# Ordering DVE and SP work in a hybrid attention/RWKV block: the next weight's lower part behind a read-out, and weight loads free of gate loads in the second branch

## The chip, the cores and the metric

The kernel runs on one core of a Trainium2 chip. A core has five engines that run side by side, each with its own instruction stream taken in order: TensorE (PE in the profile, with its weight loads as PEld), VectorE (DVE), ScalarE (ACT), GpSimd (POOL) and SyncE (SP), which here only issues DMA transfers. Data lies in HBM and is brought into the on-chip memory (SBUF) by DMA; matmuls write into the accumulator memory (PSUM). The metric is the device time of one execution in microseconds: 1654.64 us is the median of three runs before the change, with 1653.51 the lowest and 1662.36 the highest.

## The reference

One transformer-like block on a sequence of 1024 tokens of 1024 features, in float32:

```
mod = silu(c) @ w_mod + b_mod            # six shift/scale/gate vectors
u   = rms_norm(x) * (1 + scale1) + shift1
proj = u @ w_in                          # fox q,k,v,f | rwkv r,k,v,w,a,g | two gates
o_fox  = softmax(q k^T / 8 + forget decay, causal) v        # 8 heads of 64
p = p_rwkv + (token_shift(p_rwkv) - p_rwkv) * mu
o_rwkv = RWKV-7 recurrence(r, k, v, w, a, g)                # 8 heads of 64
mix = (sigmoid(p_gate0) * (o_fox @ fox_w_out) + sigmoid(p_gate1) * (o_rwkv @ rwkv_w_out)) @ w_o
h = x + gate1 * mix
h = h + gate2 * (silu(conv3(u2 @ w_up_a)) * (u2 @ w_up_b)) @ w_down
out = rms_norm(h) * final_g
```

The projections are the bulk of the work: u (1024 x 1024) times w_in (about 5,400 columns), the two output projections, w_o and the feed-forward part.

## The kernel before

**Split numbers.** Every float32 operand of a large matmul is split into a high part (rounded to the matmul's faster format) and a lower part (the rest). A product is three passes: high x high, high x low, low x high. For a weight tile the order is: weight-high with u-high (8 matmuls, one for each 128 features), weight-high with u-low (8), weight-low with u-high (8). So 24 matmuls of 512 columns make one half (512 tokens) of 128 output features, and the weight's lower part is first needed at the 17th.

**Weights, one after the other.** `load_w` (line 257 on) issues the DMA of a 128 x 1024 weight tile into a raw buffer (two of them), lets ACT copy it into the high part (L272) and DVE subtract to get the lower part in two instructions of 512 columns (L274). High and lower parts have two buffers each, so weight i+1's parts can be written while weight i is in use, once weight i-1 is through with them; the raw buffer of weight i is free for weight i+2 when its lower part is made. `Weave.step` drives this: when it makes a weight the current one, it loads the next one at once, and only then writes down the current one's matmuls.

**Users of the weights.** `shifted` makes one half of one r, k or v tile of RWKV: 24 matmuls into one of two PSUM banks (tag "big"), an ACT instruction that scales the result by mu (L366), and the read-out by DVE (L369), which adds the token-shifted part and frees the bank. Each of these 24 weight uses takes its own weight load, since the two halves are made at different times. `qk_steps` makes both halves of a q or k tile with one weight: ACT takes the high part (L393), DVE the lower part (L395, name ql), and six DMAs write them to HBM. `v_steps` uses two weight tiles at once for the attention's v, in eight 24-matmul pieces with 256 columns each, whose lower part is L955. `gate_steps` makes the gates (L337 to L342) and writes them to HBM (d_gate).

**What sets the order.** The order of PE's instructions is written out by hand over the whole kernel (`tc.manual_schedule` for PE): `Weave` has an estimated clock and puts projection matmuls between the steps of two chains, the preparation of an RWKV unit (`pre`) and its recurrence (`main`). DVE, ACT, POOL and SP are ordered in this stage by a planner that goes through the instructions in the order written, estimates when each is ready, and takes the earlier-written one among those that are ready; semaphores then follow from the data. `tc.add_manual_dep(a, b, NOSYNC)` tells the planner to put a behind b on their engine, without a semaphore. Among what DVE does beside the read-outs are 31 steps of two small operations for each RWKV unit (L784, L786) and the transposes X (L842), which wait for a DMA round trip through HBM.

**The branches.** After attention, the kernel forms gate x (output projection) for the two branches x = 0 (fox) and x = 1 (rwkv), eight tiles n each (`br_part`: 12 matmuls for each half). For tile k = 8x+n+1, `br_open` copies the weight (L1219 ACT; L1222 POOL for the lower part) and loads the gate g from d_gate (L1224, two buffers, free when DVE has used the tile two before, L1314 or L1317); `br_load` then issues the load of tile k+1's weight (L1210) into one of the two raw buffers. `after_gate` puts the load behind the last gate load in SP's order. In the second branch, w_o tiles are loaded and split too (L1287, L1258, L1259), and the last two modulation vectors are accumulated on DVE from w_mod (L1274, L1281), in both branches.

Of the kernel before, what the change touches and what calls it, by code (L numbers as in the profile page):

```python
# [12 lines left out]
ALU = mybir.AluOpType  # L13
# [5 lines left out]
NH = 512  # L19
# [16 lines left out]
NOSYNC = mybir.DependencyInfo(mybir.DependencyClass.NoSync, mybir.DependencyReason.DATA)  # L36
# [96 lines left out]
def hybrid_block(ctx: ExitStack, tc: tile.TileContext, a, out):  # L133
    nc = tc.nc
# [12 lines left out]
    def f32(ap):  # L147
        return ap.bitcast(F32)

    tt, stt, ts = nc.vector.tensor_tensor, nc.vector.scalar_tensor_tensor, nc.vector.tensor_scalar  # L150
# [15 lines left out]
    def V(name, i=0, n=1):  # L166
        o, _ = VEC[name]
        return vec[:, o + i : o + i + n]
# [13 lines left out]
    omu = cp.tile([128, 14], F32, name="omu")  # L182
# [59 lines left out]
            nc.vector.tensor_tensor(dst[:, cs], ps, bb[:, cs], op=ALU.add)  # L242

    marks = {}
    late_lo = deque()

    def lower(wait=0):

        yield wait
        if late_lo:  # L250
            hi, lo, raw = late_lo.popleft()
            for c in range(0, 1024, NH):
                tt(lo[:, c : c + NH], raw[:, c : c + NH], f32(hi[:, c : c + NH]), op=ALU.subtract)
            weave.use("DVE", weave.now, 1300)

    def load_w(src, name, pool=None, n=1024, scale=None, tags=("whi", "wlo"), bufs=2):

        pool = pool or wp
        raw = rp.tile([128, n], F32, tag="raw", name=f"raw_{name}")
        nc.sync.dma_start(raw, src)  # L260
        if scale is not None:
            nc.gpsimd.tensor_tensor(raw, raw, scale, op=ALU.mult)
        hi = pool.tile([128, n], F32R, tag=tags[0], name=f"hi_{name}", bufs=bufs)
        lo = pool.tile([128, n], F32R, tag=tags[1], name=f"lo_{name}", bufs=bufs)
        if weave.late == 1:
            i = nc.gpsimd.tensor_copy(hi, raw)
            if "head" in marks:
                tc.add_manual_dep(i.ins, marks["head"].ins.name, NOSYNC)
            late_lo.append((hi, lo, raw))
            weave.spawn(lower(9000), 0)  # L270
        else:
            nc.scalar.copy(hi, raw)  # L272
            for c in range(0, n, NH):
                nc.vector.tensor_tensor(lo[:, c : c + NH], raw[:, c : c + NH], f32(hi[:, c : c + NH]), op=ALU.subtract)  # L274
        return hi, lo

    def gemm_cm(ps, w, x, cs, nk=KT, w0=0):
# [7 lines left out]
    def gemm_steps(ps, w, x, cs, nk=KT, w0=0, by_kt=False):  # L285
        (wh, wl), (xh, xl) = w, x
        order = [(i, kt) for i in range(3) for kt in range(nk)]
        if by_kt:
            order.sort(key=lambda o: o[1])
        for n, (i, kt) in enumerate(order):  # L290
            ww, xx = ((wh, xh), (wh, xl), (wl, xh))[i]
            k0 = (w0 + kt) * 128
            mm(ps, ww[:, k0 : k0 + 128], xx[:, kt, cs], start=n == 0, stop=n == len(order) - 1)
            yield
# [29 lines left out]
    def w_in(i):  # L324
        return load_w(a["w_in"][i], f"in{i}")
# [20 lines left out]
    with ExitStack() as es:  # L346
# [4 lines left out]
        def big(name):  # L351
            return pb.tile([128, NH], F32, tag="big", name=name)
# [4 lines left out]
        def shifted(w, ti, hf, dst, prev, name, by_kt=False):  # L357

            ps = big(f"ps_{name}{hf}")
            yield from gemm_steps(ps, w, u, slice(hf * NH, hf * NH + NH), by_kt=by_kt)  # L360
            sh = shp.tile([128, NH + 1], F32, tag="sh", name=f"sh_{name}{hf}")
            if hf == 0:
                nc.vector.memset(sh[:, 0:1], 0.0)
            else:
                nc.vector.tensor_copy(sh[:, 0:1], prev)
            nc.scalar.activation(sh[:, 1 : NH + 1], ps, AF.Copy, scale=V("mu", ti))  # L366
            if hf == 0:
                nc.gpsimd.tensor_copy(prev, sh[:, NH : NH + 1])
            stt(dst, ps, omu[:, ti : ti + 1], sh[:, 0:NH], op0=ALU.mult, op1=ALU.add)  # L369

        rkv, got, last_col = {}, {}, {}

# [13 lines left out]
        def qk_steps(w, i):  # L386
            sc_ = 0.125 if i < 4 else 1.0
            for hf in range(2):
                cs = slice(hf * NH, hf * NH + NH)
                ps = big(f"qk{i}_{hf}")  # L390
                yield from gemm_steps(ps, w, u, cs)
                hi = gsp.tile([128, NH], F32R, tag="sp0", name=f"qh{i}_{hf}")
                nc.scalar.activation(hi, ps, AF.Copy, scale=sc_)  # L393
                lo = gsp.tile([128, NH], F32R, tag="sp0", name=f"ql{i}_{hf}")
                stt(lo, ps, sc_, f32(hi), op0=ALU.mult, op1=ALU.subtract)  # L395
                h0 = 2 * (i % 4)
                for t, k, r0 in ((hi, 0, 0), (lo, 0, 64), (hi, 2, 0)) if i < 4 else ((hi, 1, 0), (hi, 1, 64), (lo, 3, 0)):
                    for h in range(2):
                        nc.sync.dma_start(f32(d_st[h0 + h, k, r0 : r0 + 64, cs]), f32(t[h * 64 : h * 64 + 64, :]))
# [13 lines left out]
        with tc.tile_pool(name="st", bufs=1) as st, tc.tile_pool(name="stp", bufs=2, space=PS) as stp, \  # L413
# [126 lines left out]
            for half in range(2):  # L540
                for kt in u_steps(half):
                    low_part(kt, half, (0, 1))
                    if half == 0 and kt in (3, 5):
                        raw, hi, lo = low_raw[kt == 5]
# [13 lines left out]
        with tc.tile_pool(name="lg", bufs=1, reuse_waits="tile") as lg, \  # L558
# [108 lines left out]
            for p in range(4):  # L667
                for i in (p, 4 + p):
                    weave.add(lambda i=i: w_in(i), lambda w, i=i: qk_steps(w, i))
# [288 lines left out]
        for j in range(2):  # L958
            weave.add(lambda j=j: [load_w(a["w_v"][j, x], f"v{j}{x}") for x in range(2)], lambda w, j=j: v_steps(w, j))
# [226 lines left out]
    def bank(k, name):  # L1186
        return pb.tile([128, NH], F32, tag="big", name=name) if k > 5 else pz.tile([128, NH], F32, tag=f"p{k}", name=name)
# [16 lines left out]
    def after_gate(i):  # L1204
        if "g" in marks:
            tc.add_manual_dep(i.ins, marks["g"].ins.name, NOSYNC)

    def br_load(x, n):
        raw = br_raw[x, n] = rp.tile([128, 1024], F32, tag="raw", name=f"raw_br{x}{n}")[:, 0:NH]
        after_gate(nc.sync.dma_start(raw, a["w_br"][n, :, x * NH : x * NH + NH]))  # L1210

    def br_open(x, n):
        if (x, n) not in br_raw:
            br_load(x, n)
        raw = br_raw[x, n]
        hi = br.tile([128, NH], F32R, tag="whi", name=f"hi_br{x}{n}")
        lo = br.tile([128, NH], F32R, tag="wlo", name=f"lo_br{x}{n}")
        if x or n:
            marks["br"] = nc.scalar.copy(hi, raw)  # L1219
        else:  # L1220
            nc.gpsimd.tensor_copy(hi, raw)
        nc.gpsimd.tensor_tensor(lo, raw, f32(hi), op=ALU.subtract)  # L1222
        g = br.tile([128, S], F32, tag="g", name=f"g{x}_{n}")
        marks["g"] = nc.sync.dma_start(g, d_gate[8 * x + n])  # L1224
        opened[x, n] = (hi, lo), g
# [3 lines left out]
    if "rest" in marks:  # L1229
        g, m = (gsp.tile([128, NH], F32, tag="sp0", name=f"rest{k}") for k in range(2))  # L1230
        i = nc.scalar.activation(g, marks["rest"], AF.Abs)
# [89 lines left out]
    for x in range(2):  # L1321
        for n in range(8):
            if x or n:
                k = 8 * x + n + 1
                if k < 16:
                    br_open(k // 8, k % 8)
                if k < 15:
                    br_load((k + 1) // 8, (k + 1) % 8)
            parts = [(x, n, 0), (x, n, 1)]
            if x == 0 and n < 2:  # L1330
                parts = [(0, 0, 0), (0, 1, 0)] if n == 0 else [(0, 0, 1), (0, 1, 1)]
            for _ in range(0 if x and n > 3 else 1 if x else 2 if n < 6 else 0):
                next(mods, None)
            for part in parts:
                br_part(*part)
            if x == 0 and 1 <= n <= 4:
                rk_make((n - 1) // 2 * 2, (n - 1) % 2)
            if x == 1:
                wo_load(n)
                if n == 0:  # L1340
                    lo = [hp.tile([128, NH], F32R, tag=tag, name=f"mgl0_{k}", bufs=bufs)
                          for k, (tag, bufs) in enumerate(5 * [("xq", 5)] + 2 * [("s", 2)] + [("dg", 1)])]
                    mg_hl[0] = pairs([f"f{k}" for k in range(4)], "mgh0"), lo
                else:
                    mg_split(0, n - 1)
# [299 lines left out]
    ps = {t: [bank(k, f"wo{t}_{c}") for c, k in enumerate(ks)] for t, ks in enumerate(((0, 5), (6, 7), (1, 2)))}  # L1645
# [13 lines left out]
    def wo_do(t, k):  # L1659
        ps = [bank(k + c, f"wo{t}_{c}") for c in range(2)]  # L1660
        for kt in range(KT):
            wo_mm(t, kt, ps)
        return ps

    ps = wo_do(3, 3)
# [7 lines left out]
    ps = wo_do(4, 0)  # L1673
# [15 lines left out]
    for t, k in ((5, 2), (6, 6), (7, 4)):  # L1689
        ps = wo_do(t, k)  # L1690
# [234 lines left out]
    for s, k in enumerate(ORDER):  # L1925
        ps = banks[4:] if k in (7, 4, 2) else banks[0:4]
# [109 lines left out]
```

## Time and profile before

| what | us |
|---|---|
| median of three runs | 1654.64 |
| the profiled execution, its own time | 1657.87 |
| its span, first to last instruction | 1656.1 |
| TensorE busy in the span | 1610.4 |
| weight loads of TensorE busy | 1340.5 |
| DVE busy | 1221.4 |
| ACT busy | 821.6 |
| lower parts of w_in tiles on DVE (L274), 84 instructions | 57.7 |

The stages lie one behind the other: the first norm and the low-rank projections up to about 130 us; projections with the RWKV recurrence to about 627; attention with the last gates to 827; the two branches to 918; w_o and the second norm to about 1063; the feed-forward part to the end. In the rows of the profile, "out<-in" are the names of tiles, "x8" the number of instructions merged into a row, and "[2.78 <-DVE v L369]" says that the engine stood idle for 2.78 us just before and that the read-out of v by DVE at line 369 ended it. Idle time of an engine that is not the bottleneck costs nothing by itself. "SPq" rows are transfers at the moment that SP issues them.

### The profile page before, as it was taken

How to read it: one execution, taken by the hardware profiler on the slowest of the kernel's cores; microseconds unless marked ns; L12 is line 12 of the kernel's file. 1: busy time of each engine (PE TensorE's matmuls, PEld its weight loads, DVE VectorE, ACT ScalarE, POOL GpSimd, SP SyncE). 2: the span in 40 equal slices, each digit the busy share in tenths (PEclk: the TensorE clock that was granted, in tenths of full speed). 3: DMA queues.
4: the chain of work that ended last, by engine and by line, in shares of the span. 5: the costliest groups of instructions: out<-in, count | busy, mean ns of one | idle time of the engine just before them, and what ended most of it. 6: DMA issues, size and time to landing. Idle time of an engine off the chain costs nothing.

```text
span 1656.1 us, 25949 instructions
## 1 busy us (share of the span) xinstructions
PE 1610.4 (97%) x9694; PEld 1340.5 (81%) x9694; DVE 1221.4 (74%) x2373; ACT 821.6 (50%) x1537; POOL 133.5 (8%) x153
## 2 busy tenths in 40 slices
PE   7999999999999999999999999999999999999998
PEld 7777777897878788888887888788888888888886
DVE  5786787878876636888778447897777777886677
ACT  5563335445455655666633225644444444555455
POOL 0010101111111011221031000000000000000000
PEclk9999999999999999999999999999999999999999
DMA  9487645443333336434197421243223233674463
GB/s 337 139 322 233 178 122 140 125 122 104 100 115 97 96 114 165 125 105 124 35 358 242 184 85 43 77 134 102 96 97 119 96 99 106 212 264 157 123 210 108
DMA packets 121645, 240.59 MB, mean 145 GB/s; under 512 B 40048, under 2 KB 48880, under 8 KB 121520
## 3 DMA queue, kind: packets, MB, share of 16 engines
q1 hardware_dynamic: 113040, 220.58, 40.8%
q0 software_dynamic: 8480, 18.37, 4.2%
q8 instruction: 76, 1.25, 0.3%
q14 instruction: 49, 0.40, 0.1%
HBM read 173.35 MB, written 65.54 MB: 144 GB/s over the span
## 4 chain that ended last, share of the span: by engine, by line
PE 61%; DVE 5%; ACT 2%; DMA 2%; issue 1%; SPq 0%; POOL 0%; ACTq 0%; DVEq 0%
PE X L141 13%; PE D L141 13%; PE Y L141 6%; PE wo L141 5%; PE gt L141 5%; PE rk_ps L141 4%; PE W L141 3%; PE br L141 3%; PE lg L141 2%; PE ov L141 2%; PE tp L145 2%; PE ps_rkv L141 1%; DMA raw_wo<-in_w_o 1%; DVE nm L1049 1%; DVE P L1059 1%
## 5 line engine op out<-in xcount | busy, mean ns | idle before, releaser
L141 PE MATMUL D<-op,op 128*128 128x512 f32 x924 | 209.8, 389 | 0.0
L141 PEld LDWEIGHTS D<-op,op 128*128 128x128 f32 x924 | 173.4, 188 | 36.2 <-DVE op L1259 0.3
L141 PE MATMUL X<-T_m,S 128*128 128x512 f32 x440 | 107.8, 390 | 1.6 <-ACT T_m L1720 1.1
L141 PEld LDWEIGHTS X<-T_m,S 128*128 128x128 f32 x440 | 82.4, 188 | 20.4 <-ACT T_m L1720 2.5
L1258 ACT CAST op<-g 128x512 fp32r<-128x512 f32 x77 | 47.8, 621 | 73.7 <-PE D L141 48.8
L1259 DVE TENSOR_TENSOR op<-g,op 128x512 fp32r<-128x512 f32 x77 | 53.0, 689 | 41.3 <-ACT op L1258 41.3
L1517 DVE SCALAR_TENSOR_TENSOR c<-ab,vec,c 128x512 f32<-128x512 f32 x88 | 65.9, 750 | 18.4 <-ACT c L1520 16.8
L784 DVE TENSOR_TENSOR t<-E,M 128x60 f32<-128x60 f32 (+24 forms) x248 | 56.5, 228 | 26.5 <-DMA M<-sm 20.5
L274 DVE TENSOR_TENSOR lo_in<-raw_in,hi_in 128x512 fp32r<-128x512 f32 x84 | 57.7, 725 | 20.8 <-PE gt L141 7.2
L1483 DVE TENSOR_TENSOR A<-ur,A 128x512 fp32r<-128x512 f32 x64 | 44.0, 689 | 38.7 <-ACT A L1479 38.5
L1483 DVE TENSOR_TENSOR S<-ur,S 128x512 fp32r<-128x512 f32 x66 | 45.5, 691 | 35.2 <-ACT S L1479 35.1
L1479 ACT CAST S<-ur 128x512 fp32r<-128x512 f32 x66 | 41.0, 622 | 55.8 <-DVE ur L1472 30.6
L141 PE MATMUL Y<-T_h,A 128*128 128x512 f32 x264 | 63.7, 390 | 0.3 <-ACT T_h L1720 0.3
L141 PE MATMUL Y<-T_h,S 128*128 128x512 f32 x264 | 63.6, 390 | 0.4 <-ACT T_h L1738 0.4
L1053 ACT ACTIVATE P<-lg,nm 128x896 f32<-128x896 f32 (+3 forms) x64 | 47.5, 744 | 28.6 <-DVE nm L1049 19.6
L1479 ACT CAST A<-ur 128x512 fp32r<-128x512 f32 x64 | 39.6, 622 | 43.1 <-PE X L141 31.3
L786 DVE TENSOR_TENSOR E<-E,t 128x60 f32<-128x60 f32 (+24 forms) x248 | 55.9, 225 | 6.4
L141 PE MATMUL W<-B_f,A 128*128 128x512 f32 x252 | 60.6, 389 | 0.0
L141 PE MATMUL X<-B_b,A 128*128 128x512 f32 x252 | 60.5, 389 | 0.0
L141 PEld LDWEIGHTS Y<-T_h,S 128*128 128x128 f32 x264 | 49.5, 188 | 11.1 <-ACT T_h L1738 0.8
L141 PEld LDWEIGHTS Y<-T_h,A 128*128 128x128 f32 x264 | 49.5, 188 | 11.0 <-ACT T_h L1720 0.7
L1089 DVE TENSOR_TENSOR tl<-tp,th 128x512 fp32r<-128x512 f32 (+1 forms) x80 | 49.4, 633 | 9.2 <-ACT th L1086 8.5
(483 smaller groups left out, 4132.4 us busy)
## 6 DMA issues: line engine op xcount, KB each, us to landing
raw_in<-in_w_in SPq DMA_DIRECT2D x50, 512.0 KB, 3.9
wm<-in_w_mod SPq DMA_DIRECT2D x48, 512.0 KB, 7.2
ur<-in_w_up SPq DMA_DIRECT2D x44, 512.0 KB, 3.8
g<-d_g SPq DMA_DIRECT2D x35, 512.0 KB, 4.0
d_g<-gs SPq DMA_DIRECT2D x44, 256.0 KB, 2.0
d_g<-c SPq DMA_DIRECT2D x33, 256.0 KB, 4.5
d_st<-qh SPq DMA_DIRECT2D x64, 128.0 KB, 2.4
stA<-d_st POOLq DMA_DIRECT2D x8, 1024.0 KB, 6.7
```

The lines of the kernel that those rows point to most:

```text
L141: nc.tensor.matmul(o, lhsT, rhs, start=start, stop=stop, skip_group_check=more)
L145: nc.tensor.transpose(o, i, eye)
L274: nc.vector.tensor_tensor(lo[:, c : c + NH], raw[:, c : c + NH], f32(hi[:, c : c + NH]), op=ALU.subtract)
L784: tt(tv, E32[:, 0:J, s : s + 1].to_broadcast([128, J, W]), M32[:, s : s + 1, s + 1 : 32].to_broadcast([128, J, W]), op=ALU.mult)
L786: tt(E32[:, 0:J, s + 1 : 32], E32[:, 0:J, s + 1 : 32], tv, op=ALU.add)
L1053: nc.scalar.activation(e[:, 0:n], lg[:, 0:n], AF.Exp, bias=nm[:, 0:1], accum_out=nm[:, 1:2])
L1089: tt(tl[:, 0:w], tp[:, 0:w], f32(th[:, 0:w]), op=ALU.subtract)
L1258: nc.scalar.copy(hi, src)
L1259: tt(lo, src, f32(hi), op=ALU.subtract)
L1479: nc.scalar.copy(hi, src)
L1483: tt(lo, src, f32(hi), op=ALU.subtract)
L1517: stt(c, ab[:, x + hf * NH : x + hf * NH + NH], V("conv_w", 22 * x + i), c, op0=ALU.mult, op1=ALU.add)
```

## The change

Two edits. First: `load_w` notes the two lower-part instructions of the weight that it just loaded (`waiting`; a later load overwrites the note), and the next read-out by `shifted` or `qk_steps` puts a planner edge on each of them, so that they come behind that read-out on DVE, and clears the note. Since weight i+1 is loaded when weight i becomes current, the read-out is that of weight i's first half. Read-outs of the gates and of v put no edge. Nothing is computed differently, and no instruction is added or removed. Second: `br_load` puts the edge behind the last gate load only for x = 0; for x = 1 the weight load has no edge of that kind.

```diff
--- before.py
+++ after.py
@@ -242,7 +242,13 @@
             nc.vector.tensor_tensor(dst[:, cs], ps, bb[:, cs], op=ALU.add)
 
     marks = {}
+    waiting = []
     late_lo = deque()
+
+    def empties(i):
+        for x in waiting:
+            tc.add_manual_dep(x.ins, i.ins.name, NOSYNC)
+        waiting.clear()
 
     def lower(wait=0):
 
@@ -270,8 +276,8 @@
             weave.spawn(lower(9000), 0)
         else:
             nc.scalar.copy(hi, raw)
-            for c in range(0, n, NH):
-                nc.vector.tensor_tensor(lo[:, c : c + NH], raw[:, c : c + NH], f32(hi[:, c : c + NH]), op=ALU.subtract)
+            waiting[:] = [nc.vector.tensor_tensor(lo[:, c : c + NH], raw[:, c : c + NH], f32(hi[:, c : c + NH]), op=ALU.subtract)
+                          for c in range(0, n, NH)]
         return hi, lo
 
     def gemm_cm(ps, w, x, cs, nk=KT, w0=0):
@@ -366,7 +372,7 @@
             nc.scalar.activation(sh[:, 1 : NH + 1], ps, AF.Copy, scale=V("mu", ti))
             if hf == 0:
                 nc.gpsimd.tensor_copy(prev, sh[:, NH : NH + 1])
-            stt(dst, ps, omu[:, ti : ti + 1], sh[:, 0:NH], op0=ALU.mult, op1=ALU.add)
+            empties(stt(dst, ps, omu[:, ti : ti + 1], sh[:, 0:NH], op0=ALU.mult, op1=ALU.add))
 
         rkv, got, last_col = {}, {}, {}
 
@@ -392,7 +398,7 @@
                 hi = gsp.tile([128, NH], F32R, tag="sp0", name=f"qh{i}_{hf}")
                 nc.scalar.activation(hi, ps, AF.Copy, scale=sc_)
                 lo = gsp.tile([128, NH], F32R, tag="sp0", name=f"ql{i}_{hf}")
-                stt(lo, ps, sc_, f32(hi), op0=ALU.mult, op1=ALU.subtract)
+                empties(stt(lo, ps, sc_, f32(hi), op0=ALU.mult, op1=ALU.subtract))
                 h0 = 2 * (i % 4)
                 for t, k, r0 in ((hi, 0, 0), (lo, 0, 64), (hi, 2, 0)) if i < 4 else ((hi, 1, 0), (hi, 1, 64), (lo, 3, 0)):
                     for h in range(2):
@@ -1207,7 +1213,9 @@
 
     def br_load(x, n):
         raw = br_raw[x, n] = rp.tile([128, 1024], F32, tag="raw", name=f"raw_br{x}{n}")[:, 0:NH]
-        after_gate(nc.sync.dma_start(raw, a["w_br"][n, :, x * NH : x * NH + NH]))
+        i = nc.sync.dma_start(raw, a["w_br"][n, :, x * NH : x * NH + NH])
+        if x == 0:
+            after_gate(i)
 
     def br_open(x, n):
         if (x, n) not in br_raw:
```

## Prediction

> **What bounds the kernel now.** I read the page first, for the busy shares; then the busy time by stretch, for idle TensorE time by stage; then the waits, of TensorE and of the DMA queue; then the order of time around the places that these name. Sums are made against the profiled execution, 1657.87 us, of which the span below is 1656.1; the median of the three runs is 1654.64, so it is 3.2 us slow, and I carry differences over to the median.
>
> ```profile
> span 1656.1 us, 25949 instructions
> ...
> PE 1610.4 (97%) x9694; PEld 1340.5 (81%) x9694; DVE 1221.4 (74%) x2373; ACT 821.6 (50%) x1537; POOL 133.5 (8%) x153
> ```
>
> TensorE (PE) is busy 97%: 45.7 us are idle in all. The next rows give the stretch that the first edit touches (130 to 627 us, projections and RWKV), ten microseconds of pure projection inside it, and the second branch (871 to 918). Columns: start and end, length, then busy time and count of PE, weight loads, DVE, ACT, POOL, then clock, DMA share, GB/s.
>
> ```profile
> 130.00:140.00 10.00, 10.00 (x44) 7.93 (x43) 5.11 (x8) 3.36 (x5) 1.05 (x4) 1.00 0.87 261
> 130.00:627.00 497.00, 484.39 (x4306) 402.06 (x4305) 350.54 (x945) 237.79 (x447) 66.47 (x88) 1.00 0.46 129
> 871.00:918.00 47.00, 44.89 (x198) 36.52 (x197) 37.97 (x47) 16.75 (x24) 9.20 (x7) 1.00 0.75 259
> ```
>
> One 512-column matmul takes 10.00/44 = 0.227 us of a busy PE, back to back. PE's own order is written out by hand and is not edited, so no edit can give back more than the idle time: 497.00-484.39 = 12.6 us in the first stretch and 47.00-44.89 = 2.1 us in the second. The waits say which parts of that are within reach; three numbers: us in total, times, longest.
>
> ```profile
> PE qk L141 <- DVE v L369: 2.8, 1, 2.8
> ...
> PE br L141 <- ACT hi_br L1219: 2.1, 1, 2.1
> ...
> PE qk L141 <- DVE ql L395: 0.6, 1, 0.6
> ```
> ```profile
> SPq L260 <- DVE lo_in L274: 108.2, 29, 13.3
> ```
>
> Read-outs (L369, L395) that came late cost PE 2.8+0.6 = 3.4 us. No PE row waits for a lower part of w_in (L274). The queue row shows where lower parts bite: each weight load (L260) stands in SP's queue until the lower part that reads its buffer is done.
>
> **Part one: which lower part moves where.** When weight i starts, weight i+1 is loaded and its two lower parts are noted; the first read-out of weight i then goes ahead of them. A qk weight has two halves, so its first read-out comes 24 matmuls (5.4 us) before its successor starts, and I charge nothing there: the second half covers it. The r, k and v weights of RWKV are used for one half only, 24 matmuls in all (eight of each, row below). There the lower part of i+1 must come after all of i is read out, and i+1 needs it after 16 of its own matmuls, 16 x 0.227 = 3.6 us. That is the cover: ACT's 0.69 us, the read-out's 0.74, and one half of the lower part, 0.68, take 2.1 us if DVE is free; other matmuls woven in add cover, DVE work ahead of the read-out takes it away.
>
> ```profile
> L369 DVE SCALAR_TENSOR_TENSOR k<-ps_rkv,omu,sh_rkv x8: 734/745/751, 81.4 to 488.6; 128x512 f32<-128x512 f32 x8
> ```
> ```profile
> 201.15 0.69 ACT L366 ACTIVATE sh_rkv<-ps_rkv,vec 128x512 f32<-128x512 f32 x1 [0.80 <-PE ps_rkv L141]
> 204.82 1.29 DVE L274 TENSOR_TENSOR lo_in<-raw_in,hi_in 128x512 fp32r<-128x512 f32 x2
> 205.96 0.62 PE L141 MATMUL ps_rkv<-u_hi,lo_in 128*128 128x512 f32 x2
> 206.15 0.74 DVE L369 SCALAR_TENSOR_TENSOR k<-ps_rkv,omu,sh_rkv 128x512 f32<-128x512 f32 x1
> 206.17 0.33 SPq L260 DMA_DIRECT2D raw_in<-in_w_in  x1
> ```
>
> Here k is read out at 206.15, 5 us after its last matmul, just behind a pair of lower parts. That pair is v's, two weights on; it moves behind r's read-out and leaves k's 1.29 us earlier, at 204.82. The lower part of r, done long before until now, follows: first half at 204.82+0.66+0.68 = 206.2, due at 205.96. Stall 0.2 us. The worst place is the hand-over from v to qk:
>
> ```profile
> 216.79 0.69 ACT L366 ACTIVATE sh_rkv<-ps_rkv,vec 128x512 f32<-128x512 f32 x1 [1.30 <-PE ps_rkv L141]
> 220.19 1.75 PE L141 MATMUL qk<-u_hi,lo_in 128*128 128x512 f32 x7
> 222.50 0.43 DVE L842 STREAM_TRANSPOSE X<-TT 32x256 f32<-32x256 f32 x1 [5.07 <-DMA TT<-se]
> 222.87 1.24 DVE L274 TENSOR_TENSOR lo_in<-raw_in,hi_in 128x512 fp32r<-128x512 f32 x2
> 224.15 0.43 DVE L842 STREAM_TRANSPOSE X<-TT 32x256 f32<-32x256 f32 x1
> 224.61 0.75 DVE L369 SCALAR_TENSOR_TENSOR v<-ps_rkv,omu,sh_rkv 128x512 f32<-128x512 f32 x1
> 225.42 0.50 PE L141 MATMUL qk<-u_hi,hi_in 128*128 128x512 f32 x1 [2.78 <-DVE v L369]
> ```
>
> DVE stands 5.07 us at a transpose that waits for a DMA, and v's read-out, ready at 217.5, stands behind it. After the change the transposes end near 223.3, the read-out near 224.0, the first half of qk's lower part near 224.7, and PE stops at 220.19 instead of 222.64: 4.5 us, in place of 2.78. Net +1.7. If the planner puts the read-out ahead of the transposes instead, the place gains 2.8; I take +1.7, since the quoted order has the read-out behind both. The second such place:
>
> ```profile
> 247.17 1.28 DVE L274 TENSOR_TENSOR lo_in<-raw_in,hi_in 128x512 fp32r<-128x512 f32 x2
> 248.06 1.07 PE L141 MATMUL ps_rkv<-u_hi,lo_in 128*128 128x512 f32 x4
> 249.64 0.75 DVE L369 SCALAR_TENSOR_TENSOR k<-ps_rkv,omu,sh_rkv 128x512 f32<-128x512 f32 x1
> 250.45 0.73 PE L141 MATMUL ps_rkv<-u_hi,hi_in 128*128 128x512 f32 x2 [0.16 <-DVE k L369]
> ```
>
> k's read-out moves up by 1.28 to 248.36, the first half of r's lower part ends at 249.7, due 248.06: 1.7 less the 0.16 that goes. If the pair of r, which leaves the busy stretch ahead, shifts everything another 1.28 us, 0.2 is left. Between 0.2 and 1.5 I take 1.0.
>
> A moved lower part also holds its raw buffer longer, and so the load of the weight after next. A load lands in 3.9 us and the copy takes 1.05; with two short weights (10.9 us) between, that is covered, except where two weights are loaded for one step, as for V:
>
> ```profile
> raw_in<-in_w_in SPq DMA_DIRECT2D x50, 512.0 KB, 3.9
> ```
> ```profile
> 320.78 0.74 DVE L369 SCALAR_TENSOR_TENSOR r<-ps_rkv,omu,sh_rkv 128x512 f32<-128x512 f32 x1
> 323.37 1.05 ACT L272 CAST hi_v<-raw_v 128x1024 fp32r<-128x1024 f32 x1 [0.51 <-PE ps_rkv L141]
> 325.91 0.99 PE L141 MATMUL v<-hi_v,u_hi 128*128 128x256 f32 x7
> 330.44 0.85 PE L141 MATMUL v<-hi_v,u_hi 128*128 128x256 f32 x5 [0.30 <-DVE v L369]
> ```
>
> The second V weight takes the buffer of v, whose lower part now follows r's read-out: 321.5 to 322.8, load landed at 326.7, copy done at 327.9. PE needs it at its fifth V matmul, 325.91+0.6 = 326.5: 1.4 late, less the 0.30 at 330.44. I take 1.0, and the same for the second V step; at most 1.4 each, at least nothing. Where the lower part leaves a qk read-out (ql, 0.6 us above) that wait goes. **Part one: 1.7+1.0+0.2+2x1.0-0.6 = +4.3 us**, from -2.8-0.6 = -3.4 (plus 0.2) to 1.7+1.5+0.4+2.8 = 6.4.
>
> **Part two: the second branch's weight loads.** They may now pass the gate load ahead of them.
>
> ```profile
> 898.57 1.45 POOL L1222 TENSOR_TENSOR lo_br<-raw_br,hi_br 128x512 fp32r<-128x512 f32 x1 [5.04 <-ACT hi_br L1219]
> 906.32 0.33 SPq L1224 DMA_DIRECT2D g<-d_gate  x1
> 906.74 0.38 SPq L1210 DMA_DIRECT2D raw_br<-in_w_br  x1
> 911.21 0.62 ACT L1219 CAST hi_br<-raw_br 128x512 fp32r<-128x512 f32 x1 [1.93 <-DMA raw_br<-in_w_br]
> 911.88 2.14 PE L141 MATMUL br<-rk_m,hi_br 128*128 128x512 f32 x8 [2.11 <-ACT hi_br L1219]
> ```
>
> The last weight load goes out at 906.74, right behind a gate load, though its buffer is free from 900.0, when POOL has read it. Up to 6.7 us earlier covers the 2.11 us that PE waits: **-2.1**. On SP's queue the loads of w_o and w_mod and the gate load stand by; a gate load held behind a weight load costs at most the 0.38 of issue. The DMA share of 0.75 in this stretch leaves room. Bounds: -2.1, and +2.1 if the loads that are passed make as long a wait as goes. A rule weighed: the Trainium skill, page "DMA: Bandwidth & Descriptors", section "Issuing engines are not separate DMA queues", says that all queues' transfers share the same 16 engines and interleave; read strictly, the early load would only slow its neighbours and this part would be worth 0. The 0.75 above speaks against that, and the sum by the page would be 2.1 us higher.
>
> The sum is 4.3-2.1 = +2.2 us: 1660.1 against the profiled execution, **1657 us** against the median. Half a per cent (8.3 us) is about what a measurement of this kernel can tell from no change.
>
> **The rivals.**
> (A) The read-outs gain and nothing new waits: the planner finds room for every read-out early. 3.4 and 2.1 us go: 1654.6-5.5 = 1649. For it: no PE row waits for L274 now. Against: the 5 us lag at 201 to 206 is longer than the 3.6 us of cover.
> (B) Slower: the lower part becomes the wait of the single-half weights. Price 1.0 us each, as charged at 248; it decides from eleven of the 24 on (11 us less the 2.7 that go is 8.3). With 16 of 24: +16-2.7, 1668. For it: DVE is in order, and its lag at 206 and 224 is 5 us and more; each weight load hangs on the same lower part. Against: other matmuls woven into the 24 lengthen the cover.
> (C) The second edit does nothing, as the gate load was not what held the weight load: +4.3, 1659. Against: 906.32 and 906.74 follow each other at once.
> (D) PE has more room than its idle time, and both edits uncover it: over 8.3 us faster, at most about 12.6+2.1, 1640. The rows speak against it: 44 matmuls fill 10 us. The Trainium skill, "Perfetto Trace Analysis", section "Identifying the Most-Contended Engine", calls matmul busy time a poor measure and takes the share of weight loads instead; by the 81% above, 316 us would be open. The 0.227 us per matmul of 512 columns, with a weight load of 7.93/43 = 0.184, shows that even a full stretch reads 79% there, so here I go by the rows.
>
> **How the numbers follow.** Forecast 0.48, A 0.14, B 0.24, C 0.08, D 0.06. Forecast, A and C lie within 0.5% (0.70), B is slower (0.24), D faster (0.06). The forecast's own range is 1649 (bounds -3.2-2.1) to 1663 (6.4+2.1); the 8-in-10 range takes in B: 1648 to 1670.
>
> **What would show it.** Right: in DVE's order L274 follows L369 instead of preceding it; new PE waits for L274 near 220 and 248 and for hi_v near 326; the waits for v L369 and ql L395 gone; the row with 2.11 us at 911.88 gone and weight loads ahead of gate loads from 862 on. Wrong: PE waits for L274 at most of the 24 weights (B), or none and fewer idle us in 130 to 627 (A); a wait of PE on w_o or on gates behind 918 would undo part two. The planner's order of DVE and SP is what I cannot see; if it reorders the RWKV chain, places that I don't name will decide.

## The result and the profile after

The changed kernel takes 1674.18 us (median, 1671.36 to 1677.42), the kernel before in the same session 1657.53 us (1653.51 to 1662.36). The ratio is 1.0102, 95% interval 1.0088 to 1.0115: 1% slower. The profiled execution took 1674.64 us. Its page, the span and the busy times:

```profile
span 1672.9 us, 25928 instructions
...
PE 1615.6 (97%) x9694; PEld 1343.7 (80%) x9694; DVE 1232.5 (74%) x2373; ACT 820.0 (49%) x1537; POOL 129.1 (8%) x153
```

The work is the same; PE's instructions and their order too. The stretch that ran from 130 to 627 us now ends near 646. Busy time by stretch, changed kernel (columns as in the prediction):

```profile
130.00:646.00 516.00, 490.98 (x4304) 406.79 (x4303) 357.14 (x947) 237.13 (x448) 65.01 (x88) 0.98 0.44 125
```

PE idle there is 516.00-490.98 = 25.0 us, against 12.6 before: +12.4. PE busy for as many matmuls is 6.6 us more, at a granted clock of 0.98 instead of 1.00. Less the 2.1 us of the branches that makes +16.9, and the spans differ by 16.8. So there are two amounts to explain, and the first has its rows in PE's waits from 130 to 627 us (us in all, times, longest). After:

```profile
PE sp L141 <- ACT S L909: 7.0, 4, 2.8
PE uw L141 <- ACT TT L865: 4.0, 3, 2.1
PE qk L141 <- DVE lo_in L279: 2.7, 1, 2.7
PE q L141 <- ACT UV L816: 2.2, 1, 2.2
...
PE v L141 <- DVE lo_v L279: 1.8, 2, 1.1
...
PE tb L145 <- ACT UV L816: 0.5, 1, 0.5
```

Before, the same view had, for S and TT:

```profile
PE uw L141 <- ACT TT L859: 2.6, 2, 1.7
...
PE sp L141 <- ACT S L903: 1.4, 2, 1.0
```

S (the recurrence's state), TT and UV are small ACT copies of the RWKV chain that the edit doesn't touch. Waits for them grew by 5.6+1.4+2.7 = 9.7 us, against 12.4 us of added idle time in all. Why ACT is late shows in ACT's own waits, same stretch, after and then before:

```profile
ACT hi_in L278 <- DMA raw_in<-in_w_in: 13.2, 5, 4.2
...
ACT hi_v L278 <- DMA raw_v<-in_w_v: 8.6, 3, 3.8
```
```profile
ACT hi_in L272 <- DMA raw_in<-in_w_in: 1.0, 1, 1.0
```

ACT stood 21.8 us at high copies of weights whose load had not landed; before, 1.0 us. Two more copies, at 222.83 and 514.35 us, come after 7.2 and 5.0 us of standing that the profile puts down to DVE; their loads had gone out only at 218.54 and 509.31, and the run lower_alone below has both places under the load (6.95 and 5.13 us). The timeline after, two places:

```profile
205.91 1.28 DVE L279 TENSOR_TENSOR lo_in<-raw_in,hi_in 128x512 fp32r<-128x512 f32 x2
207.22 0.34 SPq L266 DMA_DIRECT2D raw_in<-in_w_in  x1
210.86 1.04 ACT L278 CAST hi_in<-raw_in 128x1024 fp32r<-128x1024 f32 x1 [4.16 <-DMA raw_in<-in_w_in]
211.93 1.50 ACT L816 COPY UV<-vt 64x256 f32<-64x256 f32 x4
213.48 1.15 PE L141 MATMUL q<-UV,E 64*64 64x64 f32 x32 [2.20 <-ACT UV L816]
```
```profile
410.45 0.33 SPq L266 DMA_DIRECT2D raw_in<-in_w_in  x1
414.13 1.04 ACT L278 CAST hi_in<-raw_in 128x1024 fp32r<-128x1024 f32 x1 [3.20 <-DMA raw_in<-in_w_in]
415.67 0.30 ACT L909 ACTIVATE S<-sp,pcd 128x64 f32<-128x64 f32 x1
416.02 0.43 PE L141 MATMUL sp<-S,Mt 128*128 128x64 f32 x2 [2.15 <-ACT S L909]
```

Read from top to bottom, that is the chain: the lower part, now behind the read-out, frees the raw buffer late; the load issues the moment it does; ACT stands 4.16 us at the copy; UV, next in ACT's stream, follows, and PE has waited 2.20 us for it. Five of PE's waits stand right behind such a copy, for UV at 213.48 and 328.90 and for S at 260.28, 416.02 and 524.56 us: 8.9 us in all. The 1.4 us more for TT have no late copy right ahead of them. Nobody waited for the weight itself: no PE row names a high copy.

The second edit did what was forecast: no PE row names br any more.

### The profile page after: what moved, and what is told of

The parts are those of the page before. It is cut to its first block, busy times and chain, and to the rows that moved or that the text cites. A ratio compares the mean times of both kernels' runs of the same rounds, so it can differ in the third digit from the quotient of the medians.

```text
span 1672.9 us, 25928 instructions
## 1 busy us (share of the span) xinstructions
PE 1615.6 (97%) x9694; PEld 1343.7 (80%) x9694; DVE 1232.5 (74%) x2373; ACT 820.0 (49%) x1537; POOL 129.1 (8%) x153
## 3 DMA queue, kind: packets, MB, share of 16 engines
q8 instruction: 76, 1.25, 0.3%
## 4 chain that ended last, share of the span: by engine, by line
PE 60%; DVE 5%; ACT 2%; issue 1%; DMA 0%; SPq 0%; ACTq 0%; DVEq 0%
PE X L141 13%; PE D L141 13%; PE Y L141 6%; PE wo L141 5%; PE br L141 5%; PE gt L141 4%; PE rk_ps L141 4%; PE W L141 3%; PE lg L141 2%; PE ov L141 2%; PE tp L145 2%; DVE nm L1055 1%; DVE P L1065 1%; DVE tl L1095 0%; ACT P L1059 0%
## 5 line engine op out<-in xcount | busy, mean ns | idle before, releaser
L1525 DVE SCALAR_TENSOR_TENSOR c<-ab,vec,c 128x512 f32<-128x512 f32 x88 | 65.9, 750 | 18.4 <-ACT c L1528 16.8
L278 ACT CAST hi_in<-raw_in 128x1024 fp32r<-128x1024 f32 x42 | 43.8, 1047 | 46.5 <-DMA raw_in<-in_w_in 20.6
L141 PEld LDWEIGHTS Y<-T_h,A 128*128 128x128 f32 x264 | 49.5, 188 | 10.9 <-ACT T_h L1728 0.7
```

What stands on the lines that cost most here:

```text
L141: nc.tensor.matmul(o, lhsT, rhs, start=start, stop=stop, skip_group_check=more)
L1525: stt(c, ab[:, x + hf * NH : x + hf * NH + NH], V("conv_w", 22 * x + i), c, op0=ALU.mult, op1=ALU.add)
```

## The experiments

All ratios are to the kernel before, measured in the same session.

| run | what | median us | ratio, 95% |
|---|---|---|---|
| lower_alone | first edit alone | 1677.08 | 1.0116 (1.0096 to 1.0136) |
| branch_alone | second edit alone | 1654.92 | 0.998 (0.9967 to 0.9993) |
| second_half_late | first edit, only the second of the two subtractions | 1665.5 | 1.0049 (1.0032 to 1.0066) |
| qk_only | first edit, edges at q and k read-outs | 1656.52 | 1.0003 (0.9994 to 1.0012) |
| rkv_only | edges at r, k, v read-outs | 1677.18 | 1.0125 (1.0101 to 1.015) |
| kr_edges | edges at RWKV's k and r | 1669.51 | 1.0069 (1.0047 to 1.0091) |
| v_edges | edges at RWKV's v | 1670.08 | 1.0069 (1.0048 to 1.0091) |
| pool_copy_before | before, high copy on GpSimd | 1676.89 | 1.0125 (1.0099 to 1.015) |
| pool_copy | first edit, high copy on GpSimd | 1680.97 | 1.0146 (1.0131 to 1.0162) |
| held_buffer | buffer held, lower parts early (flawed) | 1678.4 | 1.0126 (1.0101 to 1.015) |
| kr_held, v_held | the same for k and r, for v (flawed) | 1676.05, 1680.97 | 1.0125, 1.0152 |
| column_copy_4, column_copy_64 | their copy without an edge | 1685.46, 1681.93 | 1.0164, 1.0144 |
| kr_held_64, v_held_64 | held, tile of 64 bytes (flawed) | 1674.24, 1680.73 | 1.0099, 1.0136 |
| held_behind_lower | buffer held, copy ordered behind the lower parts | 1672.31 | 1.0101 (1.0083 to 1.0118) |
| qk_and_branch | edges at q and k, and second edit | 1652.68 | 0.9973 (0.9961 to 0.9985) |

The theory when they began (T1): the late load, at which ACT's stream stands, makes the loss. The rival (T2): the lower part's own lateness does.

**Each edit alone.** Each kernel is the one before with one of the two hunks of the diff.

> Part one alone: the lower parts behind the read-outs, the weight loads of the second branch as before. From the two traces, PE is 19.3 us later than before when the branches begin and gains 2.4 us in them. If the parts add up: before + 19, about 1677 us. If the second edit has a share in the loss (its loads moved the planner's order ahead of the branches): clearly less, 1665 to 1672 us.

> Part two alone: only the edge of the second branch's weight loads is taken away. If the parts add up: 2.1 to 2.4 us faster than before, the idle 2.11 us of PE before the last branch tile gone, every other wait of PE as before. If part two has a share in the loss: slower than before.

The loss is all of the first edit's, and the second gains 3 us by itself. Both theories allow that.

**Half of the lateness.** Only the second subtraction carries the edge, so half of the lower part is early and the buffer is freed a little sooner behind the read-out (the load that goes out at 207.44 us in lower_alone goes out at 206.98):

```diff
-            waiting[:] = [tensor_tensor(lo[half c], ...) for c in (0, 512)]
+            waiting[:] = [tensor_tensor(lo[half c], ...) for c in (0, 512)][1:]
```

> Part one with only the second of the two lower-part instructions ordered behind the read-out; the first, which PE needs at its 17th matmul, stays early, the second is due 4 matmuls (0.9 us) later. The raw buffer is held as long as in part one. Theory 1: most of the loss stays, 10 to 19 us over before. Theory 2: PE's waits for the lower part go almost wholly, at most 4 us over before.

ACT's wait for raw_in from 130 to 627 us, in lower_alone and then here:

```profile
ACT hi_in L278 <- DMA raw_in<-in_w_in: 26.0, 8, 7.0
```
```profile
ACT hi_in L278 <- DMA raw_in<-in_w_in: 7.8, 5, 2.6
```

Four more such waits in second_half_late, 8.9 us in all, are put down to DVE by the profile, though each copy starts 3.7 to 5.0 us after its load was issued; with them and the waits for raw_v, ACT stands 17.0 us there and at least 32.1 in lower_alone. About half of the standing, then, and less than half of the loss. The result lies between the two theories' numbers.

**Which read-outs.** qk_only drops the call of `empties` in `shifted`, rkv_only that in `qk_steps`; kr_edges and v_edges divide the second again:

```diff
-            empties(stt(dst, ps, omu[...], sh[...]))
+            out = stt(dst, ps, omu[...], sh[...])
+            if ti < 8:          # kr_edges; ti >= 8 in v_edges
+                empties(out)
```

> The first edit's edges at the q and k read-outs alone (weights with two halves each, in which the next weight's load has a whole second half to land). If the loss is ScalarE's queue standing at late loads: the two halves cover the 3.9 us of the load, few late copies, ScalarE's wait for raw_in between 130 and 627 us under 8 us against the 26.0 of the edit whole, time 1656 to 1665 us. If any lower part behind any read-out costs about the same: a third of the read-outs (8 of 32) give a quarter of the 18 us, 1662 to 1666 us.

> The first edit's edges at the r, k and v read-outs alone (24 weights with a single half each, two of which follow each other in about 11 us). If the loss is ScalarE's queue standing at late loads: nearly the whole of it is here, 1670 to 1678 us, with ScalarE's waits for raw_in of 15 us or more and PE's waits for S at 4 us or more. If any read-out costs the same: three quarters of 18 us, 1669 to 1674 us.

> The first edit's edges at the k and r read-outs alone (16 single-half weights, each with another single-half weight behind it). If the loss is the late load at which ScalarE's queue stands: the load held back here is wanted after one weight of 5.5 us, against 3.9 us of load and 1.05 us of copy, so this holds most of the loss, 1668 to 1677 us, with ScalarE's wait for the raw loads at 12 us or more and PE's waits for S at 4 us or more. If what costs is PE's wait for the lower part itself, as at the hand-over from v to q or k: little, 1655 to 1660 us.

> The first edit's edges at the v read-outs alone (8 weights; behind v comes a weight with two halves, or a step of the second V product). If the loss is the late load: the weight behind v gives the load 11 us to land, ScalarE's wait for the raw loads between 130 and 627 us stays under 8 us, 1655 to 1662 us. If what costs is PE's wait for the lower part itself: the waits of 1 to 2.7 us are all here, with the slow matmuls behind them, 1662 to 1670 us.

The q and k read-outs cost nothing, the single-half weights carry everything. That the k and r edges cost 0.7% is as T1 said. That the v edges cost as much is not: there T2 was right, with the loss at the top of its range. PE's waits in kr_edges, 130 to 640 us:

```profile
PE uw L141 <- ACT TT L867: 5.7, 3, 2.6
PE sp L141 <- ACT S L911: 4.4, 3, 2.4
PE q L141 <- ACT UV L818: 2.3, 1, 2.3
```

All three are ACT's; the lower parts themselves take three short waits there, 1.5 us in all. In v_edges the greatest is another. Timeline of DVE and PE:

```profile
222.50 0.43 DVE L850 STREAM_TRANSPOSE X<-TT 32x256 f32<-32x256 f32 x1 [5.63 <-DMA TT<-se]
...
225.37 0.75 DVE L375 SCALAR_TENSOR_TENSOR v<-ps_rkv,omu,sh_rkv 128x512 f32<-128x512 f32 x1
...
226.13 2.49 DVE L279 TENSOR_TENSOR lo_in<-raw_in,hi_in 128x512 fp32r<-128x512 f32 x4
...
226.87 1.65 PE L141 MATMUL qk<-u_hi,lo_in 128*128 128x512 f32 x3 [5.39 <-DVE lo_in L279]
```

DVE stands at a transpose, v's read-out behind it, the lower part behind that, and PE 5.39 us. This is the hand-over that the prediction named. One late load is left in v_edges (ACT stands 3.3 us, PE then 2.2 us for S). The two parts sum to 1.4%, the two together cost 1.25%: within the intervals they add up, or overlap a little.

**Another engine for the copy.** In both kernels `nc.scalar.copy(hi, raw)` becomes `nc.gpsimd.tensor_copy(hi, raw)`.

> The kernel before, with the weight's high copy on GpSimd in place of ScalarE: the control for the next run. Both theories: GpSimd's in-order queue holds little between 130 and 627 us, so between 1654 and 1666 us; ScalarE no longer has a row that waits for the raw weight's DMA.

> The first edit with the high copy on GpSimd, so that the copy that waits for the late load stands in another queue than the recurrence's ScalarE work (UV, S, TT). If the loss is ScalarE's queue standing at the copy: no ScalarE wait for the raw DMA, the PE waits for ScalarE's S between 130 and 627 us fall from 7.0 us in all to under 3, and the time is within 8 us of the control's (most of the 17 to 18 us come back); what is left is PE's wait for a lower part and whatever stands behind the copy on GpSimd. If the loss is the lower parts' own lateness, or VectorE's, the copy's engine doesn't matter: 15 to 20 us above the control.

The pair settles nothing: the control alone lost 1.25%, far from what was expected. Relative to it the first edit costs 4 us, which T1 had said, and the waits for S fell to 1.3 us, but others took their place (PE in pool_copy, 130 to 627 us):

```profile
PE q L141 <- DVE QA L817: 8.7, 2, 4.9
PE qk L141 <- DVE lo_in L279: 4.7, 1, 4.7
```

**The buffer held, the lower parts early.** Here the subtractions are where they were before, and instead a copy of one raw column gets the edge:

```diff
             nc.scalar.copy(hi, raw)
-            waiting[:] = [tensor_tensor(lo[half c], ...) for c in (0, 512)]
+            for c in (0, 512): tensor_tensor(lo[half c], ...)
+            waiting[:] = [nc.vector.tensor_copy(held, raw[:, n - 1 : n])]
```

> Before, with the lower parts early as they were, but one more tiny DVE copy (one column of the raw weight into an unused tile) ordered behind the read-out in the lower parts' place: it holds the raw buffer as long as the change does and leaves the lower parts early. Theory 1 (the buffer is freed late, the load of the weight after next goes out late, ACT stands at that weight's copy and the recurrence behind it on ACT comes late): most of part one's loss, 8 to 17 us over before, with ACT idle before L272 copies on DMA raw_in and PE waits on ACT for S and UV. Theory 2 (the lower parts themselves come late for PE, as the prediction's rival B has it): within 2 us of before. Theory 3 (the planner's other order of DVE work costs it): in between, without ACT waits on raw_in.

It lost 1.26%, which by itself would fit T1. Splitting it by read-outs broke that: both parts lost more than the same edges of the first edit in kr_edges and v_edges.

> The lower parts where they were before; behind the k and r read-outs alone VectorE copies one column of the next weight's raw buffer, so that the buffer is held as long as in the run with the k and r edges, and nothing else moves. If those edges cost 0.7% by the late load (ScalarE's queue standing at the copy, with S, UV and TT behind it): the same loss here, 1665 to 1674 us, ratio 1.004 to 1.010, ScalarE's waits for the raw loads at 12 us or more. If the lower parts' own lateness made it: 1655 to 1660 us.

> The same behind the v read-outs alone. If the v edges cost 0.7% mainly by TensorE's wait for the lower part (5.39 us at the first half of a q or k weight, and the waits for lo_v): most of the loss is gone, 1655 to 1662 us, and what is left is one late load (TensorE's wait of 2.2 us for S). If the held buffer makes it: 1664 to 1673 us.

The controls have the copies and no edge:

> The kernel before with the copy of one raw column into a tile of 4 bytes per partition, and no edge at all: nothing is held longer than the lower parts hold it. If the 4 bytes shift the tiles behind them and slow matmuls: 1663 to 1669 us (+7 to +12), in even steps from 930 us on, X<-T_m,S matmuls at 0.250 us each against 0.243. If the slope of the held runs came of their waits (heat, clock): 1654 to 1660 us.

> The same with a tile of 64 bytes, so that the tiles behind it keep their place within 64 bytes: the control of the next two. The copy itself is 39 times about 0.06 us on VectorE. 1654 to 1660 us, and no slope behind 930 us, if the shift was the cause; as slow as with 4 bytes if the copies are.

> Lower parts where they were; the raw buffer held behind the k and r read-outs by the copied column, with a tile of 64 bytes. If those edges' 0.7% is the late load: ratio 1.004 to 1.008, 1662 to 1670 us, with PE's waits for S, UV and TT as in the k and r run. If the lower parts' own lateness made most of it: under 1.003, up to 1661 us.

> The same behind the v read-outs. If the v edges' 0.7% is mainly TensorE's wait for the lower part: under 1.004, up to 1662 us, with one late load left. If the held buffer makes it there too: 1.005 to 1.009, 1664 to 1671 us.

The copies alone cost 1.4 to 1.6%, at least as much as with the edges, so none of these five held runs says anything of T1. One reason is in DVE's waits of column_copy_64 (130 to 640 us):

```profile
DVE held L282 <- DMA raw_in<-in_w_in: 32.1, 22, 3.7
DVE held L282 <- DMA raw_v<-in_w_v: 9.8, 4, 4.5
```

The copy reads only the raw buffer, so the planner put it ahead of the subtractions, and DVE stood at it for the load: the same fault as ACT's, made by the experiment. The other reason, the new tile itself, is told in the last section.

The next run orders the copy behind the subtractions and writes into a tile that is there already:

```diff
+            held = top[:, 0:1]                                    # the existing tile
+            tc.add_manual_dep(copy.ins, last_subtraction.ins.name, NOSYNC)
```

> Lower parts where they were before; behind them, and behind the q, k, r and v read-outs, VectorE copies one column of the raw buffer, so that the buffer is held as in the edit and nothing else is late. No new tile. If the late load carries the loss alone: 1672 to 1678 us, ratio 1.009 to 1.013. If it carries the k and r edges' share (0.7%) and a late load or two at the v edges, and the lower part's own lateness the rest: 1664 to 1671 us, ratio 1.004 to 1.009, PE's waits for S at 4 us or more, none for a lower part over 1 us. If only the lower part's own lateness counts: 1655 to 1661 us. Matmuls X<-T_m,S back at 0.243 us each.

1.0101 (1.0083 to 1.0118). The interval reaches into the first two of the ranges expected. The ratio and the 1672.31 us lie in the first, the late load carrying the loss alone (1.009 to 1.013, 1672 to 1678 us), the time at its lower edge. ACT's and PE's waits, 130 to 640 us:

```profile
ACT hi_in L278 <- DMA raw_in<-in_w_in: 15.1, 9, 3.2
...
ACT hi_v L278 <- DMA raw_v<-in_w_v: 10.0, 4, 3.9
```
```profile
PE sp L141 <- ACT S L911: 4.8, 4, 2.1
PE v L141 <- DVE vs L963: 3.6, 4, 1.8
PE uw L141 <- ACT TT L867: 3.5, 3, 2.0
PE q L141 <- ACT UV L818: 3.3, 1, 3.3
PE qk L141 <- DVE top L281: 2.1, 1, 2.1
```

No PE wait for a lower part is left, ACT stands 25.1 us at late loads, and most or all of the first edit's loss (1.0116, 1.0096 to 1.0136) is there. Five of PE's waits, for UV and S, stand right behind a copy that waited for its load, as in the whole edit: 8.0 us here, 8.9 there. Two rows, 2.4 us in all, are put down to the added copy (top; the second is 0.3 us) and belong to the experiment. The same copy without the edges was not run, so what its 39 instructions of 0.14 us cost by themselves is not measured; no DVE row waits at one. So the held buffer is enough to make nearly the whole loss; the lower part's lateness makes a loss of its own where only the v edges stand; in the whole edit the two are not additive, and how much each has of its 1.0 to 1.2% stays open. The v edges with the buffer held but the lower parts early were run only in the flawed form.

**A version that beats both.** The edges at q and k alone, with the second edit:

> The edges at the q and k read-outs alone, and the change's second edit with them: the two parts that cost nothing or gained. Against the kernel before, 0 for the edges (1.0003 measured) and -0.2% for the loads: 1652 to 1656 us, ratio 0.997 to 0.999. If the two gains exclude each other (the edges move the last read-out on the way to the branches): 1655 to 1658 us.

0.9973 (0.9961 to 0.9985), 4.5 us faster than before. Whether the q and k edges add anything to the second edit alone (0.998, 0.9967 to 0.9993) is not shown.

## Why the prediction was wrong, point by point

**The failed step** is this one: "A load lands in 3.9 us and the copy takes 1.05; with two short weights (10.9 us) between, that is covered". It asked only when PE needs the weight, and for PE it was covered: no PE row waits for a high copy. It left out what stands behind the waiting copy on ACT. The load at 207.22 came in time for its weight and 4.16 us too late for ACT's stream. Charged at nothing, the late loads cost PE 8.9 us of idle time in five waits for S and UV, and hold up the hand-over from v to qk as well (next point). In held_behind_lower, where the lower parts are early, a buffer held as long is enough for nearly the whole loss.

**The hand-over from v to qk, +1.7:** not there in the whole edit. PE waits 2.69 us in place of 2.78, and by another path than the one forecast:

```profile
218.54 0.40 SPq L266 DMA_DIRECT2D raw_in<-in_w_in  x1
220.14 0.43 DVE L848 STREAM_TRANSPOSE X<-TT 32x256 f32<-32x256 f32 x1
222.83 1.05 ACT L278 CAST hi_in<-raw_in 128x1024 fp32r<-128x1024 f32 x1 [7.20 <-DVE bon L833]
223.78 0.68 ACT L372 ACTIVATE sh_rkv<-ps_rkv,vec 128x512 f32<-128x512 f32 x1
224.82 0.74 DVE L375 SCALAR_TENSOR_TENSOR v<-ps_rkv,omu,sh_rkv 128x512 f32<-128x512 f32 x1
```

The transposes are done at 220.57, so they hold nothing up. v's read-out waits for its scaling by ACT (sh_rkv), and that stands behind a high copy whose load went out at 218.54. The lower part that frees this load's buffer came behind r's read-out and ended at 216.12, and SP issued other transfers first. So it is the late load again, this time by way of ACT, then DVE, to PE. Where the v edges stand alone the chain is the one forecast, and there PE waits 5.39 us in place of 2.78, +2.6.

**The second place, +1.0 at 248, and +0.2 at 206:** absent. No PE row names lo_in for r, k or v weights in the changed kernel. PE's loss at that time is the wait for S of 2.8 us at 260.28.

**V, 2 x 1.0:** right in size, 1.8 us in two waits, though PE waited for the lower part (lo_v) and not for the late high copy.

**ql, -0.6:** the wait at 188.57 us is gone, as forecast; a new one of 0.28 us has come at 154.40.

**Part two, -2.1:** right. The wait of 2.11 us is gone, and branch_alone measured 0.998.

**Rival B** had the sign and nearly the size (1668), by a mechanism that did not occur: 16 waits of 1.0 us for lower parts. There is one of 2.7 us and two for V. Its row, "each weight load hangs on the same lower part", was the right one and was followed to PE instead of to ACT. Rival D is out: PE's idle time went up and the time with it.

**Left out altogether:** 6.6 us of slower matmuls behind PE's new pauses (last section).

## What to carry to other kernels

When an instruction that frees a buffer is moved back, follow the freed buffer to its load, the load to the instruction that stands waiting for it, and then read what is queued behind that instruction on its in-order engine; whether the matmul unit gets its operand in time is only half of the question. Delay the release only where the next user of the buffer has a long cover (the two-half q and k weights here: ratio 1.0003, against 1.0125 for the single-half ones). And give an experiment that adds an instruction its control without the cause under test before believing it: here the added copy alone cost more than what it was to show.

## What the runs showed of the hardware that was not expected

**A pause of PE can be followed by some 3 us at half its clock, or not.** Busy time by stretch, behind the pause of 2.69 us at 226.21 and that of 2.84 us at 260.28 (after), and behind the 2.78 us at 225.42 (before); the clock is the third number from the end:

```profile
226.20:229.30 3.10, 3.09 (x8) 2.49 (x9) 2.79 (x13) 0.00 (x0) 0.01 (x1) 0.55 0.39 135
260.30:263.40 3.10, 3.10 (x11) 2.52 (x11) 0.00 (x0) 0.77 (x2) 0.00 (x0) 0.56 0.41 156
```
```profile
225.40:228.00 2.60, 2.58 (x14) 1.88 (x16) 2.10 (x9) 0.86 (x2) 0.17 (x1) 1.00 0.59 190
```

```profile
226.21 3.10 PE L141 MATMUL qk<-u_hi,lo_in 128*128 128x512 f32 x7 [2.69 <-DVE lo_in L279]
```

These seven matmuls took 3.10 us after the pause and 1.75 us before the change (0.44 and 0.25 us each). Shorter pauses came ahead of half clock too, and not at once:

```profile
342.80:345.80 3.00, 3.00 (x12) 2.81 (x13) 2.97 (x10) 1.76 (x4) 0.19 (x1) 0.50 0.53 180
417.80:420.80 3.00, 3.00 (x10) 2.42 (x9) 2.85 (x6) 0.31 (x1) 0.48 (x2) 0.50 0.62 123
```
```profile
285.80:288.80 3.00, 3.00 (x20) 2.54 (x19) 2.93 (x10) 1.12 (x3) 0.61 (x2) 0.50 0.86 292
```

The first two are the changed kernel, 2.4 and 1.8 us after pauses of 1.10 us (up to 340.43) and 2.15 us (up to 416.02); the third is the kernel before, 1.3 us after one of 1.73 us (up to 284.54). In steps of 0.4 us, the changed kernel shows five stretches of about 3.4 us at 0.50 between 130 and 646 us (from about 226.5, 260.8, 294.8, 342.5 and 417.6), the kernel before one. Four more, each costing half its length, make about 6.8 us by this estimate. The Trainium skill, "TensorE: Matmul & The Clock Gate", section "What's actually happening", has the clock halved after an idle window of about 3.4 us that runs freely; the halved clock agrees, but these pauses are shorter than the window, and of pauses of 2.7 to 2.8 us two were followed by 0.55 and 0.56 and one by 1.00. The 2.20 us at 213.48 were followed by 1.00 as well. What decides was not tested. The bill here is the 6.6 us above: behind a wait of 1 to 3 us, another 1.7 us can be lost.

**A new tile went with slower matmuls elsewhere.** With a new tile of 4 or 64 bytes per partition, in front of others, one group of feed-forward matmuls that has nothing to do with it was slower; the Y groups stayed at 0.240 us. Groups of PE from 1060 to 1660 us in before, column_copy_4, column_copy_64 and held_behind_lower (no new tile); busy time over count gives 0.243, 0.252, 0.250 and 0.243 us:

```profile
L141 PE MATMUL X<-T_m,S 128*128 128x512 f32 x400 | 97.3, 389 | 0.5 <-ACT x L1557 0.5
```
```profile
L141 PE MATMUL X<-T_m,S 128*128 128x512 f32 x416 | 104.9, 397 | 1.3 <-ACT T_m L1728 1.1 <-ACT x L1565 0.2
```
```profile
L141 PE MATMUL X<-T_m,S 128*128 128x512 f32 x413 | 103.3, 395 | 0.2 <-ACT x L1565 0.2
```
```profile
L141 PE MATMUL X<-T_m,S 128*128 128x512 f32 x408 | 99.3, 389 | 0.5 <-ACT x L1565 0.5
```

That the shifted addresses do it was not shown directly; that it goes with the new tile, of either size, and is gone without it, was.
